# A two-layer decoder trunk: a first group of four outputs, other loads, an input order with two groups ahead of the up-projections, and scores on 128 rows

## The chip, the cores and the metric

The kernel runs on one core of a Trainium2 chip, in one launch for the whole trunk. The metric is the device time of that launch in microseconds (us), the median of several runs.

## The reference

The trunk has 2 layers; the batch is 1, the sequence 256 positions, the model width 2048, all in float32. Cut to what matters here, a layer is:

```python
h = rmsnorm(x, g_mix)
z = h @ w_in
zq, zkv, zkr, sc_b, sc_c, sc_h, cf_a, cf_g, rq, rk, rv, rg = split_cols(z, ...)
y_a = attention(zq, zkv, zkr)
y_b = sc_b * causal_dwconv(sc_c * sc_h, w_sc)
u   = causal_dwconv(cf_a * sigmoid(cf_g), w_cf, b_cf)
y_c = silu(layernorm(u))
y_d = silu(rg) * rmsnorm(retention(rotate(rq), rotate(rk), rv))
x = x + concatenate([y_a, y_b, y_c, y_d]) @ w_o
uf = causal_dwconv(rmsnorm(x) @ w_up, w_ffn_conv)
x = x + (silu(gate) * up) @ w_down
x = x + (p @ w_pe) * sigmoid(rmsnorm(x) @ w_pg)
```

The attention first makes low-rank inputs: q comes from a norm of zq (512 columns) and `w_q_up`, k and v from a norm of zkv (256) and `w_kv_up`. Each of its 4 heads has 128 columns without position and 64 that are rotated by it; the rotated 64 of k come from zkr and are the same for all heads. A score is thus a product over 128 + 64 numbers. A retention head, 4 of them too, has q and k of 64 rotated numbers, and its scores are multiplied by a decay table. `w_cf` has 31 taps on 512 channels.

## The kernel before

**Layout and precision.** Everything is kept with channels on the 128 partitions and the 256 positions along the free axis. A float32 product is made of three: weights and inputs are each split in a rounded part `hi` and a rest `lo`, and hi x hi, hi x lo and lo x hi are summed in PSUM. An input tile S holds its hi half in columns 0 to 255 and its lo half in columns 256 to 511. So each 128x128 block of weights is used twice (`linear`, line 308): its `hi` by one matmul of 512 columns, its `lo` by one of 256. An output of 128 channels of the input projection takes 16 blocks.

**The weight stream.** The host writes all blocks in the order of their use, as `in_groups` and the loops of line 50 on give it. They come 16 at a time, 1 MB a load, in three buffers `raw`. ACT casts 8 blocks at once to `hi` (`conv_hi`, line 262, three buffers), and DVE subtracts that from `raw` to give `lo` (`conv_lo`, line 276, five buffers). `use` (line 293) is called ahead of each matmul and issues the conversions that the buffers have room for, so that the order of the matmuls sets the order of the conversions on ACT and DVE.

**The groups.** `in_groups` (line 88) lists the groups of the input projection: four pairs cf0 to cf3 (a half of `cf_a` with its gate), zkv, zkr, zq0, zq1, then "up" (the up-projections, `do_up`, line 593), rk, rq, rv, rg0, rg1, and the short convolution's. A group makes two outputs (zkr one, rv four) in one accumulator of two PSUM banks; there are two of these and four single banks `ps` for everything else. In layer 0, cf0 runs while x arrives: `pre` (line 856) splits two input tiles at a time, as `norm_split` (line 485 on) writes it, and squares them for the norm of line 485 on. `evac` (line 366) brings an accumulator out: ACT copies one half, DVE adds the other and multiplies by the norm's row.

**Side work.** What lies between the groups is written as generators in chains of `Bg` (line 146): chain A holds the attention with its norms and the tables of cosines and sines (`rope_tables`, line 438), C the 31 taps of each tile of the convolution, R the retention, N the first norm. `linear` calls `bg.tick()` after each step of two blocks per output, and a tick lets each chain go a step of its rate on: 1 for most, 0.4 for C (`CF_RATE`), 0.25 for the tables, which also wait for eight ticks first. Each instruction so issued stands in its engine's queue behind the last matmul or `lo` conversion issued before it, and the queues run in that order. All DVE instructions and matmuls go through `Paced` and show as line 135 in the profile.

**Scores.** `rope` (line 472) rotates: ACT copies the halves crosswise, DVE multiplies both by the tables and adds. The rotated k of zkr is made twice, on rows 0 to 63 and 64 to 127 (the group's columns are doubled, line 90), since the tile `qr` holds two heads, one on each half of the rows. `t_attn` (line 628) makes a head's scores in two pieces, of 128 and 256 columns, each of two float32 matmuls, one on 128 rows and one on the 64 of its head:

```python
T.matmul(ps[:, c0:c0 + n], qn[j][:, s, qs], kn[j][:, s, 0:n], start=True, stop=False)
T.matmul(ps[:, c0:c0 + n], qr[pr, j, qs], kr[pr, 0, 0:n], start=False, stop=True)
```

`t_ret` (line 774) makes a retention head's in two matmuls on 64 rows each. For the norm of k, `t_zkr` (line 559) squares rows 0 to 63 alone.

**First loads.** They are issued from line 215 on. SP's queue takes 8 KB of `vt` (the vectors of gains and taps; these columns are the gains of the first norm), then the first weights and the 8 tiles of x, 512 KB and 256 KB each, in turn. POOL's queue takes `ident`, the positions, `ropec`, the other 466 KB of `vt` and the decay table `dect`.

Of the kernel before, what the change touches and what calls it, by code (L numbers as in the profile page):

```python
# [17 lines left out]
P = 128  # L18
# [17 lines left out]
GRP = 32  # L36
NHI, NLO = 3, 5
# [50 lines left out]
def in_groups():  # L88
    r = lambda a: np.arange(a, a + P)
    rd = np.concatenate([np.arange(O_ZKR, O_ZKR + 64)] * 2)  # L90
    out = [("cf%d" % i, [r(O_CA + i * P), r(O_CG + i * P)]) for i in range(4)]
    out += [("zkv", [r(O_ZKV), r(O_ZKV + P)]),
            ("zkr", [rd]),
            ("zq0", [r(O_ZQ), r(O_ZQ + P)]),
            ("zq1", [r(O_ZQ + 2 * P), r(O_ZQ + 3 * P)]),
            ("up", None),
            ("rk", [r(O_RK), r(O_RK + P)]),
            ("rq", [r(O_RQ), r(O_RQ + P)]),
            ("rv", [r(O_RV + i * P) for i in range(4)]),
            ("rg0", [r(O_RG), r(O_RG + P)]),  # L100
            ("rg1", [r(O_RG + 2 * P), r(O_RG + 3 * P)])]
# [86 lines left out]
def trunk(ctx: ExitStack, tc: tile.TileContext, ws, xT, pT, pos, vec, dec, ident_d, rope_c, out):  # L188
# [25 lines left out]

    vt = one.tile([P, L * NV], F32, tag="vt", name="vt")
    nc.sync.dma_start(vt[:, 0:KD], vec[:, 0:KD])
    st = {"dma": 2, "hi": 0, "lo": 0, "b": 0, "uh": 0, "ul": 0}
    raws, his, los = {}, {}, {}
    NRAW = 3
    raws[0] = tl("raw", [P, CB * P], F32, NRAW, wp)  # L220
    x = [one.tile([P, 2, S], F32, tag="x%d" % i, name="x%d" % i) for i in range(8)]
    raws[1] = tl("raw", [P, CB * P], F32, NRAW, wp)
    for kind, i in (("w", 0), ("x", 0), ("w", 1), ("x", 1), ("x", 2), ("w", 2), ("x", 3), ("x", 4), ("w", 3),
                    ("x", 5), ("x", 6), ("x", 7)):
        if kind == "x":
            nc.sync.dma_start(x[i], xT[i])
        else:
            o = slice(i % 2 * HB * P, (i % 2 + 1) * HB * P)
            nc.sync.dma_start(raws[i // 2][:, o], ws[i // 2][:, o])
# [9 lines left out]
    ones = one.tile([P, P], F32, tag="ones", name="ones")  # L239
    V.memset(ones, 1.0)  # L240
# [19 lines left out]


    def conv_hi(h):
        h = min(h, nhalf - 1)
        while st["hi"] <= h:
            i = st["hi"]
            while st["dma"] <= min(i // 2 + 1, ws.shape[0] - 1):
# [205 lines left out]
    def rope(dst, src, n, ct, sn, tag):  # L472

        sw = tl(tag, [P, n, S], F32, 3)
# [3 lines left out]
        V.tensor_tensor(dst, src, bc(ct, n), op=ALU.mult)  # L478
        V.tensor_tensor(dst, dst, sw, op=ALU.add)
# [47 lines left out]
    def layer_fwd(li, nrm, a, nxt):  # L527
# [31 lines left out]
        def t_zkr(z):  # L559
            sq = tl("krsq", [64, S], F32)  # L560
            A.activation(sq, z[0:64, 0], AF.Square)
# [4 lines left out]
            kr = tl("kr", [P, 1, S], F32)  # L566
            rope(kr, kg, 1, tabs["cm"], tabs["sm"], "m")
# [60 lines left out]
        def t_attn(ksq, qsq, qrsq, kn, vv, qn, qg):  # L628
# [4 lines left out]
            col_sums(psk, 8, [st_["krsq"]])  # L633
# [33 lines left out]
            for hh in range(4):  # L667
# [6 lines left out]
                pr = slice(64 * s, 64 * s + 64)  # L674
# [386 lines left out]
```

## Time and profile before

| what | value |
|---|---|
| time, median of 3 runs | 2411.74 us (2410.95 to 2411.9) |
| the profiled execution's own time | 2411.2 us |
| its span, first to last instruction | 2409.4 us |
| PE (matmul) busy | 2386.6 us, 99% |
| DVE busy | 1752.0 us, 73% |
| ACT busy | 1316.6 us, 55% |
| POOL busy | 10.7 us |
| moved by DMA | 443.33 MB, mean 184 GB/s |
| weights `hi`: matmuls of 512 columns in `linear` | 6560, busy 1543.5 us |
| weights `lo`: matmuls of 256 columns in `linear` | 6432, busy 841.3 us |
| `lo` conversions on DVE, 128x1024 | 830, busy 1000.8 us |

The page gives each engine's busy time over the span, and the groups of instructions that cost most. A busy share is an average over all stages. The views of the trace that are quoted below cut it in time: the list of waits says for what an engine stood idle and how long, the timeline gives start and length of runs of like instructions on an engine. In a timeline matmuls overlap, since a matmul starts before the one ahead has ended; so time is read there from start to start.

### The profile page before, as it was taken

The numbers are of one execution on the slowest core, as the hardware profiler recorded it, in microseconds if no ns is written. First come the engines' busy times: TensorE is split into PE (matmuls) and PEld (weight loads), VectorE is DVE, ScalarE is ACT, GpSimd is POOL, SyncE is SP. The second block draws the span as 40 slices with busy tenths as digits, with TensorE's granted clock in tenths as the row PEclk, the third lists the DMA queues.
The fourth block names the chain that finished last, engine by engine and source line by source line (L and its number), as shares of the span: only waits on it lengthen the run. The fifth ranks groups of instructions, "written<-read, shape, count | busy, mean of one in ns | idle before, by whom it ended". The sixth has DMA issues, their size and how long they took to land.

```text
span 2409.4 us, 34651 instructions
## 1 busy us (share of the span) xinstructions
PE 2386.6 (99%) x13808; PEld 2101.9 (87%) x13808; DVE 1752.0 (73%) x2722; ACT 1316.6 (55%) x1896; POOL 10.7 (0%) x35
## 2 busy tenths in 40 slices
PE   8999999999999999999999999999999999999999
PEld 7888888888888888888989888888888888888888
DVE  7977977777656777666788779777775567776665
ACT  6665565555445555555556665655554455555453
POOL 0000000000000000000000000000000000000000
PEclk9999999999999999999999999999999999999999
DMA  6533555555555555555554444555555555555554
GB/s 242 180 141 144 177 191 192 180 198 182 192 192 186 199 177 196 188 190 186 185 189 174 157 145 175 192 191 183 191 188 193 191 188 189 186 191 191 192 187 146
DMA packets 63332, 443.33 MB, mean 184 GB/s; under 512 B 7249, under 2 KB 7505, under 8 KB 10305
## 3 DMA queue, kind: packets, MB, share of 16 engines
q1 hardware_dynamic: 62640, 439.39, 50.8%
q8 instruction: 108, 1.77, 0.3%
q0 software_dynamic: 528, 1.73, 0.2%
q14 instruction: 56, 0.45, 0.1%
HBM read 438.99 MB, written 2.10 MB: 183 GB/s over the span
## 4 chain that ended last, share of the span: by engine, by line
PE 93%; DVE 4%; ACT 1%; issue 1%; DMA 1%; SPq 0%; POOLq 0%; ACTq 0%; DVEq 0%
PE acc L135 90%; PE ps L135 4%; DVE lo L135 2%; DVE cfu L135 1%; DMA x<-xT 0%; DVE s L135 0%; DVE e L135 0%; ACT dg L426 0%; DMA m<-pT 0%; ACT hi L272 0%; DVE S L135 0%; ACT m L476 0%; DVE m L135 0%; DVE x L135 0%; ACT e L369 0%
## 5 line engine op out<-in xcount | busy, mean ns | idle before, releaser
L135 PE MATMUL acc<-S,hi 128*128 128x512 f32 x6560 | 1543.5, 387 | 12.1 <-DVE S L135 10.8
L135 PEld LDWEIGHTS acc<-S,hi 128*128 128x128 f32 x6560 | 1203.7, 188 | 241.7 <-DVE S L135 11.3
L135 DVE TENSOR_TENSOR lo<-raw,hi 128x1024 fp32r<-128x1024 f32 x830 | 1000.8, 1220 | 205.1 <-ACT hi L272 169.9
L272 ACT CAST hi<-raw 128x1024 fp32r<-128x1024 f32 x830 | 872.1, 1053 | 357.3 <-PE acc L135 311.2
L135 PE MATMUL acc<-S,lo 128*128 128x256 f32 x6432 | 841.3, 283 | 1.3 <-DVE lo L135 1.3
L135 PEld LDWEIGHTS acc<-S,lo 128*128 128x128 f32 x6432 | 817.5, 192 | 23.1 <-DVE lo L135 1.9
L369 ACT COPY e<-acc 128x512 f32<-128x512 f32 x138 | 80.5, 584 | 417.9 <-PE acc L135 417.6
L135 DVE TENSOR_TENSOR e<-acc,e 128x512 f32<-128x512 f32 x138 | 94.9, 688 | 259.0 <-ACT e L369 258.9
L135 DVE SCALAR_TENSOR_TENSOR m<-e,vt,m 128x255 f32<-128x255 f32 (+1 forms) x352 | 146.1, 477 | 0.0
L904 ACT COPY e<-acc 128x512 f32<-128x512 f32 x64 | 37.6, 587 | 147.0 <-PE acc L135 147.0
L135 DVE TENSOR_TENSOR x<-x,acc 128x512 f32<-128x512 f32 x64 | 44.0, 688 | 99.8 <-ACT e L904 99.8
L135 DVE SCALAR_TENSOR_TENSOR cfu<-cfpad,vt,cfu 128x256 f32<-128x256 f32 x240 | 115.3, 481 | 1.6
L135 DVE TENSOR_TENSOR e<-e,rrow 128x512 f32<-128x512 f32 x138 | 94.8, 687 | 4.4
L942 ACT ACTIVATE m<-e,vt 128x256 f32<-128x256 f32 x176 | 79.5, 500 | 0.0
L135 DVE TENSOR_TENSOR S<-m,S 128x256 fp32r<-128x256 f32 x92 | 38.9, 425 | 40.5 <-ACT S L380 40.5
L380 ACT CAST S<-m 128x256 fp32r<-128x256 f32 x92 | 37.2, 406 | 53.5 <-DVE m L135 53.5
L135 DVE TENSOR_TENSOR x<-x,e 128x512 f32<-128x512 f32 (+1 forms) x82 | 55.6, 677 | 2.2
L426 ACT ACTIVATE dg<-ident,s8r 128x128 fp32r<-128x128 f32 x104 | 33.4, 391 | 31.3 <-DVE s8r L135 31.3
L135 PE MATMUL acc<-hi,S 128*128 128x512 f32 x144 | 47.4, 398 | 0.0
L384 ACT ACTIVATE S<-x,vt 128x256 fp32r<-128x256 f32 x96 | 42.9, 496 | 1.7 <-DMA x<-xT 1.6
L135 DVE SCALAR_TENSOR_TENSOR S<-x,vt,S 128x256 fp32r<-128x256 f32 x96 | 42.0, 479 | 0.9 <-ACT S L384 0.9
L947 ACT ACTIVATE m<-m 128x256 f32<-128x256 f32 x88 | 36.0, 410 | 3.7 <-DVE m L135 3.7
(161 smaller groups left out, 693.7 us busy)
## 6 DMA issues: line engine op xcount, KB each, us to landing
raw<-ws SPq DMA_DIRECT2D x413, 1024.0 KB, 4.8
raw<-ws SPq DMA_DIRECT2D x4, 512.0 KB, 9.5
x<-xT SPq DMA_DIRECT2D x8, 256.0 KB, 10.1
out<-x SPq DMA_DIRECT2D x7, 256.0 KB, 3.7
dect<-dec POOLq DMA_DIRECT2D x1, 512.0 KB, 9.8
m<-pT POOLq DMA_DIRECT2D x4, 128.0 KB, 3.5
vt<-vec POOLq DMA_DIRECT2D x1, 466.0 KB, 8.3
out<-x SPq DMA_DIRECT2D x2, 128.0 KB, 1.7
```

Of the source, the lines that this page charges most:

```text
L135: r = fn(*a, **k)
L272: A.copy(his[i], raws[i // 2][:, (i % 2) * HB * P:(i % 2 + 1) * HB * P])
L369: A.copy(out_, t[:, 0:nmt, S:2 * S])
L380: A.copy(dst[:, 0:S], src)
L384: A.activation(dst[:, 0:S], src, AF.Identity, scale=g)
L426: A.activation(dg[:, i, tt], ident, AF.Identity, scale=hl[i][:, c0 + tt:c0 + tt + 1])
L904: A.copy(e, t[:, :, S:2 * S])
L942: A.activation(y[:, m], u[:, m], AF.Identity, scale=w(2))
L947: A.activation(y[:, 0], y[:, 0], AF.Silu)
```

## The change

It does six things.

1. The first group makes the four outputs of cf0 and cf1 at once (`cf01`), two in an accumulator and two in single banks `ps`; in layer 0 a step is one input tile and four weight blocks, and the squares of the first norm come two tiles at a time, half of them after the group.
2. The groups cf2 and cf3 come behind zq1, ahead of the up-projections.
3. `WARM` = 12 matmuls of `ones` by `ones`, whose results are never read, are the first on PE.
4. The 8 KB of `vt` go alone on POOL's queue. SP's queue takes first 4 blocks of weights, the two halves of the first x tile, 4 more blocks, then x tiles and weights in turn, and behind them `ident`, `ropec`, the rest of `vt` and the positions; `dect` follows with the sixth conversion. The first 8 blocks are converted in two pieces of 4.
5. The tables wait for six ticks and then go a step every tick.
6. The rotated q of retention and the rotated k of attention are written to two tiles, one with rows 64 to 127 zero, one with rows 0 to 63 zero (POOL fills them), and all scores are products over 128 rows. The squares of zkr run on 128 rows, and the sum over them takes a column of `ropec` that selects half.

```diff
+WARM = 12
 def in_groups():
-    out = [("cf%d" % i, [r(O_CA + i * P), r(O_CG + i * P)]) for i in range(4)]
-    out += [("zkv", [r(O_ZKV), r(O_ZKV + P)]),
-            ("zkr", [rd]),
...
-            ("zq1", [r(O_ZQ + 2 * P), r(O_ZQ + 3 * P)]),
-            ("up", None),
+    cf = lambda i: [r(O_CA + i * P), r(O_CG + i * P)]
+    out = [("cf01", cf(0) + cf(1)),
+           ("zkv", [r(O_ZKV), r(O_ZKV + P)]),
+           ("zkr", [rd]),
...
+           ("zq1", [r(O_ZQ + 2 * P), r(O_ZQ + 3 * P)]),
+           ("cf2", cf(2)),
+           ("cf3", cf(3)),
+           ("up", None),
...
+    V.memset(ones, 1.0)
     vt = one.tile([P, L * NV], F32, tag="vt", name="vt")
-    nc.sync.dma_start(vt[:, 0:KD], vec[:, 0:KD])
+    nc.gpsimd.dma_start(vt[:, 0:KD], vec[:, 0:KD])
...
+    load_w(0, 4)
+    for m in range(2):
+        nc.sync.dma_start(x[0][:, m], xT[0][:, m])
+    load_w(4, 8)
+    for i in range(1, 6):
+        nc.sync.dma_start(x[i], xT[i])
+        load_w(8 * i, 8 * i + 8)
+    for i in range(6, 8):
+        nc.sync.dma_start(x[i], xT[i])
...
-    nc.gpsimd.dma_start(ident, ident_d)
+    nc.sync.dma_start(ident, ident_d)
-    nc.gpsimd.dma_start(ropec, rope_c)
-    nc.gpsimd.dma_start(vt[:, KD:], vec[:, KD:])
+    nc.sync.dma_start(ropec, rope_c)
+    nc.sync.dma_start(vt[:, KD:], vec[:, KD:])
+    nc.sync.dma_start(posi, pos.broadcast_to([P, S]))
...
-    nc.gpsimd.dma_start(dect, dec)
...
+    for _ in range(WARM):
+        wm = pst()
+        T.matmul(wm[:, 0:P], ones, ones, start=True, stop=True)
...
+    def pieces(i):
+        n = HB * P // (2 if i == 0 else 1)
+        return [slice(j, j + n) for j in range(0, HB * P, n)]
+    def c_first(i):
+        return i == 5
...
+            if c_first(i):
+                nc.sync.dma_start(dect, dec)
             his[i] = tl("hi", [P, HB * P], F32R, NHI, wp)
-            A.copy(his[i], raws[i // 2][:, (i % 2) * HB * P:(i % 2 + 1) * HB * P])
+            for o in pieces(i):
+                A.copy(his[i][:, o], src(i)[:, o])
...
     def rope(dst, src, n, ct, sn, tag):
         V.tensor_tensor(sw, sw, bc(sn, n), op=ALU.mult)
-        V.tensor_tensor(dst, src, bc(ct, n), op=ALU.mult)
-        V.tensor_tensor(dst, dst, sw, op=ALU.add)
+        if isinstance(dst, list):
+            V.tensor_tensor(src, src, bc(ct, n), op=ALU.mult)
+            for q, d in enumerate(dst):
+                r = slice(64 * q, 64 * q + 64)
+                G.memset(d[64 - 64 * q:128 - 64 * q], 0.0)
+                V.tensor_tensor(d[r], src[r], sw[r], op=ALU.add)
+        else:
+            V.tensor_tensor(dst, src, bc(ct, n), op=ALU.mult)
+            V.tensor_tensor(dst, dst, sw, op=ALU.add)
...
-            col_sums(psk, 8, [st_["krsq"]])
+            col_sums(psk, 8, [(st_["krsq"], ropec[:, 3:4])])
...
-                    T.matmul(ps[:, c0:c0 + n], qr[pr, j, qs], kr[pr, 0, 0:n], start=False, stop=True)
+                    T.matmul(ps[:, c0:c0 + n], qr[:, j, qs], kr[:, s, 0:n], start=False, stop=True)
...
-                T.matmul(ps[:, 0:S], rk[pr, j, 0:P], rq[pr, j, :], start=True, stop=True)
-                T.matmul(ps[:, S:384], rk[pr, j, P:S], rq[pr, j, P:S], start=True, stop=True)
+                T.matmul(ps[:, 0:S], rk[:, j, 0:P], rq[s][:, j, :], start=True, stop=True)
+                T.matmul(ps[:, S:384], rk[:, j, P:S], rq[s][:, j, P:S], start=True, stop=True)
...
+            if kind == "cf01":
+                t = pacc.tile([P, 2, 512], F32, tag="acc", name=nm("acc"))
+                t2 = [pst(), pst()]
+                linear(h, 4, AB_IN, ps=[t[:, 0, :], t[:, 1, :]] + t2, pre=pre)
...
-                    bg.add("A", 0.25, wait_ticks(8))
-                    bg.add("A", 0.25, rope_tables())
+                    bg.add("A", 1, wait_ticks(6))
+                    bg.add("A", 1, rope_tables())
```

**First place: the start of PE's queue.** `acc` are accumulators, `ps` single banks, S_0, S_1 the first split input tiles; x2 stands for two matmuls of the row. Before:

```order
L1056 UNCONDITIONAL_BRANCH
L135 MATMUL acc_140<-S_0_4_123,hi_145 128x512 x2
L135 MATMUL acc_140<-S_0_4_123,lo_153 128x256 x2
L135 MATMUL acc_140<-S_1_5_124,hi_145 128x512 x2
L135 MATMUL acc_140<-S_1_5_124,lo_153 128x256 x2
L135 MATMUL acc_140<-S_2_6_125,hi_145 128x512 x2
L135 MATMUL acc_140<-S_2_6_125,lo_153 128x256 x2
```

With the change:

```order
L1102 UNCONDITIONAL_BRANCH
L139 MATMUL ps_126<-ones 128x128
L139 MATMUL ps_128<-ones 128x128
...
L139 MATMUL ps_148<-ones 128x128
L139 MATMUL acc_167<-S_0_16_150,hi_174 128x512 x2
L139 MATMUL ps_168<-S_0_16_150,hi_174 128x512
L139 MATMUL ps_169<-S_0_16_150,hi_174 128x512
L139 MATMUL acc_167<-S_0_16_150,lo_181 128x256 x2
L139 MATMUL ps_168<-S_0_16_150,lo_181 128x256
L139 MATMUL ps_169<-S_0_16_150,lo_181 128x256
L139 MATMUL acc_167<-S_1_17_151,hi_174 128x512 x2
```

The unused matmuls stand ahead, and each input tile now serves four matmuls of each kind in place of two, before the next tile is wanted.

**Second place: DVE's queue in the groups behind the convolution's first.** `lo` are the conversions that PE waits for, `cfu` the taps, `e` evacuations, `tab...` the tables, m and s temporaries. Before, in cf2 and zkv:

```order
L135 TENSOR_TENSOR lo_488<-raw_428,hi_470 128x1024
L135 SCALAR_TENSOR_TENSOR cfu_60_350<-cfpad_107,vt,cfu_60_350 128x256 x6
L135 TENSOR_TENSOR e_518<-acc_427,e_518 128x512
L135 SCALAR_TENSOR_TENSOR cfu_60_350<-cfpad_107,vt,cfu_60_350 128x256
L135 TENSOR_TENSOR e_518<-e_518,rrow_318 128x512
L135 SCALAR_TENSOR_TENSOR cfu_60_350<-cfpad_107,vt,cfu_60_350 128x256
L135 TENSOR_TENSOR lo_530<-raw_456,hi_528 128x1024
L135 SCALAR_TENSOR_TENSOR cfu_60_350<-cfpad_107,vt,cfu_60_350 128x256
L135 TENSOR_TENSOR cfpad_111<-e_518,c_522 128x256
L135 SCALAR_TENSOR_TENSOR cfu_60_350<-cfpad_107,vt,cfu_60_350 128x256
L135 TENSOR_TENSOR lo_543<-raw_456,hi_541 128x1024
```

With the change, in zkr and zq0:

```order
L139 TENSOR_TENSOR e_584<-acc_451,e_584 128x512
L139 TENSOR_TENSOR tabsr<-tabcr,m_547 128x256
L139 TENSOR_TENSOR e_584<-e_584,rrow_432 128x512
L139 TENSOR_SCALAR tabcr<-tabsr 128x256
L139 TENSOR_TENSOR lo_593<-raw_481,hi_591 128x1024
L139 TENSOR_SCALAR m_547<-tabcr 128x256
L139 TENSOR_SCALAR tabsr<-tabsr 128x256
L139 TENSOR_TENSOR tabcr<-tabcr,m_547 128x256
L139 TENSOR_SCALAR tabsm<-tabsm,ropec 128x256
L139 TENSOR_SCALAR tabcr<-tabcr 128x256
L139 TENSOR_TENSOR m_601<-m_601 128x256
L139 TENSOR_SCALAR tabsr<-tabsr,ropec 128x256
```

The rows of the tables, which stood one by one between conversions and taps, now stand several in a row between two conversions.

**Third place: PE's queue ahead of the up-projections.** `acc_966` before is zq1, `acc_1028` with the change cf3; S_4_131 and S_4_112 are the first tiles of the normed zkv, which the up-projection of k and v reads. Before:

```order
L135 MATMUL acc_966<-S_10_14_133,lo_971 128x256 x2
L135 MATMUL acc_966<-S_11_15_134,lo_971 128x256 x2
L135 MATMUL acc_1097<-S_4_131_860,hi_1007 128x256 x2
L135 MATMUL acc_966<-S_12_16_135,lo_992 128x256 x2
L135 MATMUL acc_966<-S_13_17_136,lo_992 128x256 x2
L135 MATMUL acc_966<-S_14_18_137,lo_992 128x256 x2
L135 MATMUL acc_966<-S_15_19_138,lo_992 128x256 x2
L135 MATMUL acc_966<-S_15_19_138,hi_990 128x512 x2
L135 MATMUL acc_1097<-S_4_131_860,lo_1009 128x256
L135 MATMUL acc_1097<-S_4_131_860,hi_1007 128x256 x2
L135 MATMUL acc_1097<-S_4_131_860,lo_1009 128x256
```

With the change:

```order
L139 MATMUL acc_1028<-S_12_28_162,lo_1045 128x256 x2
L139 MATMUL acc_1028<-S_13_29_163,lo_1045 128x256 x2
L139 MATMUL acc_1028<-S_14_30_164,lo_1045 128x256 x2
L139 MATMUL acc_1028<-S_15_31_165,lo_1045 128x256 x2
L139 MATMUL acc_1028<-S_15_31_165,hi_1043 128x512 x2
L139 MATMUL acc_1126<-S_4_112_670,hi_1058 128x256 x2
L139 MATMUL acc_1126<-S_4_112_670,lo_1060 128x256
L139 MATMUL acc_1126<-S_4_112_670,hi_1058 128x256 x2
```

The same step now comes behind cf3, two groups after zq1, and its `lo` matmuls no longer stand behind matmuls of zq1.

## Rows read from the trace of the kernel before

**Rows 1.** The page: the span, and PE's busy time, share and instructions.
```profile
span 2409.4 us, 34651 instructions
...
PE 2386.6 (99%) x13808; PEld 2101.9 (87%) x13808; DVE 1752.0 (73%) x2722; ACT 1316.6 (55%) x1896; POOL 10.7 (0%) x35
```

**Rows 2.** PE's waits, 0 to 125 us: us in total, times, longest.
```profile
PE acc L135 <- DVE S L135: 10.8, 3, 8.5
PE acc L135 <- DVE lo L135: 1.3, 2, 1.1
PE acc L135 <- ACT S L604: 1.3, 1, 1.3
PE ps L135 <- DVE m L135: 1.2, 1, 1.2
```

**Rows 3.** Timeline of PE from 8 us: start, length, line, operation [idle before].
```profile
8.53 1.22 PE L135 MATMUL acc<-S,hi 128*128 128x512 f32 x2 [8.53 <-DVE S L135]
...
13.49 1.22 PE L135 MATMUL acc<-S,hi 128*128 128x512 f32 x2 [2.03 <-DVE S L135]
...
17.48 0.63 PE L135 MATMUL acc<-S,hi 128*128 128x512 f32 x2
...
18.96 0.64 PE L135 MATMUL acc<-S,hi 128*128 128x512 f32 x2
...
19.67 0.62 PE L135 MATMUL acc<-S,hi 128*128 128x512 f32 x2
```

**Rows 4.** Stretch 10 to 20 us: length, busy PE, PEld, DVE, ACT, POOL, clock, DMA, GB/s.
```profile
10.00:20.00 10.00, 7.97 (x31) 6.57 (x31) 7.86 (x14) 8.38 (x16) 0.00 (x0) 1.00 1.04 403
```

**Rows 5.** DVE's waits, 43 to 120 us.
```profile
DVE cfpad L135 <- ACT c L721: 1.2, 1, 1.2
DVE s L135 <- PE ps L135: 0.4, 1, 0.4
DVE S L135 <- ACT S L384: 0.4, 1, 0.4
DVE m L135 <- PE ps L135: 0.4, 1, 0.4
```

**Rows 6.** Timeline of all engines from the start.
```profile
0.84 0.17 DVE L135 MEMSET ones<- 128x128 f32 x1 [0.84 <-PEq L1051]
...
8.00 0.87 DVE L135 SCALAR_TENSOR_TENSOR S<-x,vt,S 128x256 fp32r<-128x256 f32 x2
...
38.10 6.99 PE L135 MATMUL acc<-S,hi 128*128 128x512 f32 x30
```

**Rows 7.** DMA issues, 0 to 30 us: count, KB each, median us to landing.
```profile
vt<-vec POOLq DMA_DIRECT2D x1, 466.0 KB, 8.3
...
ident<-ident POOLq DMA_DIRECT2D x1, 64.0 KB, 4.9
vt<-vec SPq DMA_DIRECT2D x1, 8.0 KB, 1.7
```

**Rows 8.** Timeline of PE: attention scores, then retention; float32 matmuls have two records each.
```profile
194.82 0.38 PE L135 MATMUL ps<-S,S 128*128 128x128 f32 x2
...
196.80 0.73 PE L135 MATMUL acc<-S,hi 128*128 128x512 f32 x2
...
206.43 0.92 PE L135 MATMUL ps<-m,S 128*128 128x256 f32 x4
207.10 0.70 PE L135 MATMUL acc<-S,hi 128*128 128x512 f32 x2
...
207.73 0.92 PE L135 MATMUL ps<-S,S 64*128 64x256 f32 x4
208.58 0.96 PE L135 MATMUL acc<-S,hi 128*128 128x512 f32 x3
```

**Rows 9.** Timeline of DVE from 59.8 us, layer 0.
```profile
59.80 1.22 DVE L135 TENSOR_TENSOR lo<-raw,hi 128x1024 fp32r<-128x1024 f32 x1
60.94 0.29 DVE L135 TENSOR_SCALAR m<-m 128x256 f32<-128x256 f32 x1
61.14 0.48 DVE L135 SCALAR_TENSOR_TENSOR cfu<-cfpad,vt,cfu 128x256 f32<-128x256 f32 x1
61.53 0.42 DVE L135 SCALAR_TENSOR_TENSOR tabsm<-m,m 128x256 f32<-128x256 f32 x1
61.87 0.48 DVE L135 SCALAR_TENSOR_TENSOR cfu<-cfpad,vt,cfu 128x256 f32<-128x256 f32 x1
```

More of the change, by code (lines that the diff above doesn't have):

```diff
@@ L212, in pst @@
         return pmis.tile([P, 512], F32, tag="ps", name=nm("ps"))
+    ones = one.tile([P, P], F32, tag="ones", name="ones")
+    V.memset(ones, 1.0)
     vt = one.tile([P, L * NV], F32, tag="vt", name="vt")
-    nc.sync.dma_start(vt[:, 0:KD], vec[:, 0:KD])
-    st = {"dma": 2, "hi": 0, "lo": 0, "b": 0, "uh": 0, "ul": 0}
+    nc.gpsimd.dma_start(vt[:, 0:KD], vec[:, 0:KD])
+    st = {"dma": 3, "hi": 0, "lo": 0, "b": 0, "uh": 0, "ul": 0}
     raws, his, los = {}, {}, {}
     NRAW = 3
-    raws[0] = tl("raw", [P, CB * P], F32, NRAW, wp)
@@ L221, in trunk @@
     x = [one.tile([P, 2, S], F32, tag="x%d" % i, name="x%d" % i) for i in range(8)]
[L222 to L229, printed above, removed]
+    for i in range(3):
+        raws[i] = tl("raw", [P, CB * P], F32, NRAW, wp)
@@ L232, in trunk @@
-    posi = tl("e", [P, S], I32, 3)
-    nc.gpsimd.dma_start(posi, pos.broadcast_to([P, S]))
+    nc.sync.dma_start(ident, ident_d)
     ropec = one.tile([P, 5], F32, tag="ropec", name="ropec")
-    nc.gpsimd.dma_start(ropec, rope_c)
-    nc.gpsimd.dma_start(vt[:, KD:], vec[:, KD:])
+    nc.sync.dma_start(ropec, rope_c)
+    nc.sync.dma_start(vt[:, KD:], vec[:, KD:])
+    tabs = {}
+    for nme in ("cm", "sm", "cr", "sr"):
+        tabs[nme] = one.tile([P, S], F32, tag="tab" + nme, name="tab" + nme)
@@ L237, in trunk @@
+    posi = tabs["sr"].bitcast(I32)
+    nc.sync.dma_start(posi, pos.broadcast_to([P, S]))
     dect = one.tile([P, 4, S], F32, tag="dect", name="dect")
-    nc.gpsimd.dma_start(dect, dec)
-    ones = one.tile([P, P], F32, tag="ones", name="ones")
-    V.memset(ones, 1.0)
     ones_r = one.tile([P, P], F32R, tag="ones_r", name="ones_r")
@@ L565, in t_zkr @@
             yield
-            kr = tl("kr", [P, 1, S], F32)
-            rope(kr, kg, 1, tabs["cm"], tabs["sm"], "m")
+            kr = tl("kr", [P, 2, S], F32)
+            rope([kr[:, q:q + 1] for q in range(2)], kg, 1, tabs["cm"], tabs["sm"], "m")
             st_["kr"] = kr
@@ L851, in layer_fwd, with pre @@
             n = len(cols)
[L852 to L866 removed]
+            if kind == "cf01":
+                pre = None
+                if li == 0:
+                    def pre(k):
+                        if k % 2 == 0:
+                            norm_split(nrm, k // 2)
+                            if k >= 8:
+                                norm_square(nrm, (k - 8) // 2)
+                t = pacc.tile([P, 2, 512], F32, tag="acc", name=nm("acc"))
+                t2 = [pst(), pst()]
+                linear(h, 4, AB_IN, ps=[t[:, 0, :], t[:, 1, :]] + t2, pre=pre)
+                if li == 0:
+                    for i in range(4, 8):
+                        norm_square(nrm, i)
+                    bg.add("N", 1, norm_end(nrm))
+                bg.flush("N")
+                if li == 0:
+                    bg.add("A", 1, wait_ticks(6))
+                    bg.add("A", 1, rope_tables())
+                zs = [evac_in(t, 2, AB_IN), tl("e", [P, 2, S], F32, 3)]
+                for m in range(2):
+                    evac(t2[m][:, None, :], 1, AB_IN, zs[1][:, m:m + 1], nrm.row)
+                for i in range(2):
+                    for _ in t_glu(zs[i], i):
+                        pass
+                    bg.add("C", CF_RATE, t_cf(i))
+                continue
+            t = linear(h, n, AB_IN)
             if kind in ("rg0", "rg1"):
```

47 lines of the change are left out of this document (18 added, 29 removed).

## The prediction, made before the changed kernel ran

> **What bounds the kernel now.** The page first: TensorE (PE) is busy for 2386.6 of the 2409.4 us of the span [rows 1], so the time is PE's queue, and only what shortens that queue or fills a hole in it counts. The holes come next, from PE's list of waits: up to 125 us it waits 10.8 us for the split of the input, 1.3 for `lo` conversions, 1.3 for ScalarE (ACT) at line 604 and 1.2 for a VectorE (DVE) sum [rows 2]. Third, the timeline of PE's start: the first matmul runs at 8.53 us, there is a hole of 2.03 us before 13.49, and the steps are slow until 17.48 [rows 3]. A step is two 512-column and two 256-column matmuls: 18.96 to 19.67 is 0.71 us, while the three steps from 13.49 to 17.48 took 1.33 each. So a block (one matmul of each width) costs 0.357 us at the 2.4 GHz level and nearly twice that at the 1.2 GHz level, although the window from 10 to 20 us gives the granted clock as 1.00 [rows 4]. Before it rose, PE had worked without a hole from 13.49 on. Last, DVE: from 43 to 120 us it waits for 2.4 us in all, once for 1.2 and three times for 0.4 [rows 5]. There DVE runs as its queue is written, and that is where a faster start can be lost again.
>
> **Part 1, the start.** Before, DVE makes the `lo` half of the first x tile from 8.00 us on [rows 6], behind the conversion of 1024 weights per partition, and the first matmul waits for it. The change cuts these pieces in half and puts only them at the head of SP's queue, takes the tables off POOL's queue, and leaves 8 KB of vt there. From POOL the rest of vt took 8.3 us to land beside the loads of x [rows 7]. The small vt is the first on POOL's queue now, but no row shows how long it alone takes from there: no less than the 1.7 us that SP's small vt took, no more than the 8.3 of the long one [rows 7]. Nearest is ident, 64 KB, first on that queue, 4.9 us, and vt is smaller, so I take 4: issued at 1.2, there at 5.3. ACT 0.45, DVE about 0.5 and the hand-overs put the first matmul at 6.4 us, 2.1 earlier (3.9 and 9.5 to 10 at the ends).
>
> Twelve unused matmuls fill PE from the memset of `ones` (0.84 + 0.17) on [rows 6]. In f32, which the trace lists as two records a matmul, 384 columns took 0.67 us at the full rate (206.43 to 207.10 [rows 8]), so 128 cost 0.22, so 0.43 at half: they reach to about 6.2 if the clock stays low and end sooner if it rises; either way PE has worked for 4 to 5 us by 6.4. I take the whole slow stretch as gone. Its price: five slow steps, two from 8.53 on and three from 13.49 on, at 1.33 in place of 0.71, 3.1 us. (Nothing of it gone is the other end.)
>
> With four outputs a weight block feeds as before, but each x tile now feeds twice the work: 8 blocks, 2.86 us of PE. In the 10 us from 10 on ACT was busy 8.38 and DVE 7.86 [rows 4], in which about four x tiles and their weights were prepared, some 2.1 us a tile. So they keep up after the second x tile, where I count 1.2 us of waiting for the second conversion in place of the hole of 2.03 [rows 3]. The 64 blocks cost 22.8 us. Before, the third group began at 38.10 [rows 6], with 1.2 us of the norm's small matmuls and waits in it that now come later. After: 6.4 + 22.8 + 1.2 = 30.4. **Gain 38.1 - 1.2 - 30.4 = 6.5 us.**
>
> **Part 2, DVE takes some back.** The rope tables went one step every fourth tick and now go every tick, all inside DVE's work for zkr and zq0 (second place of the order). Start to start a conversion costs DVE 1.14 us, a tap 0.39, a table instruction 0.20 or 0.34 [rows 9]. From the norm's last sum to zq0's fourth conversion its queue now holds 8 conversions (9.1 us), 33 table instructions (8.7), 12 taps (4.8), 13 evacuations and gates priced likewise (5.3) and small ones (1.9): 29.8 us without waits. I add 4 us for waits: 0.6 for the copy out of PSUM, 1.3 for the norm's sums, 0.6 for its row, 1.5 for the sigmoid and its table load (the same chain cost 1.2 at the sigmoid before [rows 5]). Begun at 29.4, this ends at 63.5 to 64. PE wants that conversion at 30.4 + 0.5 (the norm's small matmuls) + 11.4 (zkv, 32 blocks) + 5.7 (zkr) + 6.8 + 2.9 (zq0) = 57.7. It is 6 us late, and the order gives PE only six `hi` matmuls of the next group meanwhile (1.4 us, of which 0.4 only shifts). **Loss 5.2 us.** Later DVE is ahead again: zq1 to cf3 are 12 conversions in 31.7 us of DVE's queue against 34.3 us of PE.
>
> **Part 3, the waits before the up-projections.** Between zq1 and kv now stand cf2 and cf3, 22.9 us of PE work (third place), so zkv's and zq's norms are done when the up-projections want them. The four waits, 1.3 + 1.3 + 1.2 us [rows 2], go: **gain 3.8 us**. Late next: zkv's row inside zq1, whose diagonal DVE finishes at about 67.8, a wait of up to 1 us; and ACT at the up-projections, for which PE waited at line 604 before [rows 2] and which has the last two evacuations of cf3 on its queue besides. I take off 0.1 here and keep 2 us for the range. In layer 1 there are no tables and no start to make up; I count nothing there. Sum of parts 1 to 3: 6.5 - 5.2 + 3.8 - 0.1 = 5.0 us.
>
> **Part 4, scores on 128 rows.** A head's scores go 128 rows, 64, 128, 64: from 194.82 to 196.80, 1.98 us, and the next 512-column matmul takes 0.11 more than its 0.23 [rows 8]: 2.09 us for 768 columns. The product with the values, 384 columns all on 128 rows, takes 0.68 (206.43 to 207.10) and 0.09 after it; 384 more columns, without another entry or exit, I put at 0.64. So all on 128 rows a head costs 1.41 us by these rows. Per switch of row count about 0.2 us goes: 0.1 in the matmul before it, 0.1 in the one after. I take 0.62 rather than 0.68 a head, for entry waits that stay: 8 heads, 5.0 us. A retention head on 64 rows: 207.73 to 208.58 and 0.11 after, 0.96 against 0.77: 0.2 x 8 = 1.6 us. DVE gets one more instruction at each of four ropes (0.34 to 0.6), POOL six fills; both queues are idle enough there. **Gain 6.6 us**; ends 0 (the switch costs nothing of its own) and 7.5.
>
> The Trainium skill, TensorEngine Tiling, section Key Properties, says that a change of tiling mode drains TensorE; its section When to Use Tiling recommends two row tiles where the contracted size is 64 or less, for up to twice the speed, and by that this part would lose. The trace sides with the first: 384 columns on 64 rows take 0.85 us, on 128 rows 0.68 [rows 8].
>
> The dect load and vt's rest go through SP behind x: 5 MB ahead of them, and in the window from 10 to 20 us 403 GB/s moved [rows 4]; even at half that rate they are there by 30, before their first readers. The mask column for krsq costs nothing, the late taps (6 fewer by the up-projections) end before the last half of the output projection.
>
> **Sum.** 5.0 + 6.6 = 11.6 us off the profiled execution's 2411.2: 2399.6. The runs' median, 2411.74, is 0.5 higher, so the forecast is **2400 us**.
>
> **Rivals.**
> (a) DVE's table work is hidden after all, since it may use the holes that I count as waits, or the weight buffers hold enough: part 2 costs nothing, 2395 us. For it: five `lo` buffers are 14 us of PE work. Against: DVE had no slack there before either.
> (b) DVE takes the whole start: waits for sigmoid, sine and row add up to 10 us, or vt lands late at the first step. Then only part 4 is left, 2411.7 - 6.6 = 2405.
> (c) The switch of rows is not what the extra 0.1 us are; part 4 gives nothing: 2406.7.
> (d) Slower: a 64-row product is the cheaper one, and zeros on the other rows double it. Each of the 16 heads has 384 columns of it, 0.85 us [rows 8]: 13.6 us more, part 4's gain gone, parts 1 to 3 kept: 2411.7 + 13.6 - 5.0 = 2420. It decides from 0.31 us per head on (5.0 / 16). Rows 8 speak against it. Only the advice above, from the Trainium skill's TensorEngine Tiling, would have it so.
> (e) The start does not move, since vt on POOL's queue lands as late as the long one did: first matmul at 10, part 1 falls to about 3 us and part 2 with it: 2401 to 2403, inside the range.
>
> **How the numbers follow.** The forecast's case with (e) 0.60, (a) 0.15, (b) 0.17, (c) 0.06, (d) 0.02. A measurement of this kernel tells about 0.2%, 4.8 us, from no change: 2406.9. (c) lies on that line, so two thirds of it go to no change: faster 0.94, the same 0.04, slower 0.02. The range takes in (a) with part 4 at its upper end, 2394, and (b), 2405; it leaves out (c), (d) and the tails, under 2 in 10.
>
> **What would show it.** First real matmul near 6.4 and steps of 1.43 us for four blocks from the start; the third group, zkv, at about 30.4; PE waiting for `lo` 4 to 6 us between 54 and 66; no waits of over 0.5 us at the up-projections; a head's scores in 1.3 to 1.5 us. Wrong if zkv starts later than 33, if the `lo` waits in zq0 are under 2 or over 8 us, or if a head still takes 1.9.

## The result, and the profile after

The changed kernel takes 2398.77 us (median of 6 runs, 2398.28 to 2399.71), the kernel before 2411.73 in the same comparison: 0.9947 of it, 95% interval 0.9935 to 0.996. It is 13.0 us faster; 2400 was forecast, 2394 to 2405 the range. The profiled execution took 2398.78 us, its span is 2397.0. So the total came within 1.2 us. Its parts did not all come so, and the rest of this document is about them.

The page of the changed kernel, its span and its busy times:

```profile
span 2397.0 us, 34732 instructions
...
PE 2381.7 (99%) x13832; PEld 2107.2 (88%) x13832; DVE 1752.7 (73%) x2731; ACT 1318.8 (55%) x1900; POOL 11.6 (0%) x39
```

Against [rows 1] the span is 12.4 us shorter, of which PE's busy time gives 4.9 and its idle time the rest; the 5.3 us of unused matmuls count as busy here. PE's list of waits up to 125 us shows what idle time is left:

```profile
PE acc L139 <- DVE e L139: 4.7, 2, 4.4
PE acc L139 <- ACT hi L298: 2.0, 1, 2.0
PE ps L139 <- DVE ones L139: 1.1, 1, 1.1
```

Of the four lines of [rows 2] none is left at its place: the first wait for the split of the input is filled by unused matmuls (1.1 us until `ones` is set), and the waits for `lo`, for the row sum and for ACT at line 604 (now 639) are gone. New is a wait of 4.4 us for `e`, an evacuation on DVE. The timeline of PE's start:

```profile
1.06 5.28 PE L139 MATMUL ps<-ones 128*128 128x128 f32 x24 [1.06 <-DVE ones L139]
6.11 0.71 PE L139 MATMUL acc<-S,hi 128*128 128x512 f32 x2
...
11.13 0.74 PE L139 MATMUL acc<-S,hi 128*128 128x512 f32 x2 [1.98 <-ACT hi L298]
...
13.08 1.05 PE L139 MATMUL acc<-S,hi 128*128 128x512 f32 x2
...
15.64 0.90 PE L139 MATMUL acc<-S,hi 128*128 128x512 f32 x2
...
17.32 0.63 PE L139 MATMUL acc<-S,hi 128*128 128x512 f32 x2
```

The first matmul that counts runs at 6.11 us (8.53 before, [rows 3]). The unused ones reach until 6.1, at the low level throughout (24 records, 0.22 us each from start to start, twice the 0.11 of a 128-column record at the full rate). The first two steps, of four blocks each, run at full rate from 6.11 to 8.98. Then PE stands idle for 1.98 us, and the step at 13.08 takes 2.56 us where one from 17.32 on takes 1.40: the clock has fallen again. The windows (their columns as in [rows 4], the granted clock is the third figure from the end) say so too, and once more behind the long wait at 50 us:

```profile
11.00:17.00 6.00, 5.82 (x22) 4.66 (x23) 5.89 (x9) 6.00 (x13) 0.00 (x0) 0.72 1.04 402
17.00:30.00 13.00, 13.00 (x78) 11.41 (x77) 11.65 (x18) 9.21 (x15) 0.00 (x0) 1.00 0.96 360
...
55.00:62.00 7.00, 7.00 (x22) 5.57 (x22) 5.48 (x14) 2.30 (x4) 0.00 (x0) 0.60 0.00 0
```

The long wait itself, in PE's timeline, and what DVE does meanwhile:

```profile
32.74 1.98 PE L139 MATMUL acc<-S,hi 128*128 128x512 f32 x8
...
44.45 0.63 PE L139 MATMUL acc<-S,hi 128*128 128x512 f32 x2
...
50.15 0.39 PE L139 MATMUL acc<-S,hi 128*128 128x512 f32 x1
54.96 6.77 PE L139 MATMUL acc<-S,hi 128*128 128x512 f32 x17 [4.42 <-DVE e L139]
61.57 0.50 PE L139 MATMUL ps<-ones,m 128*128 128x1 f32 x4
```

```profile
45.84 1.36 DVE L139 TENSOR_TENSOR e<-e,rrow 128x512 f32<-128x512 f32 x3
48.45 0.43 DVE L139 TENSOR_TENSOR cfpad<-e,c 128x256 f32<-128x256 f32 x1 [1.26 <-ACT c L755]
...
54.13 0.69 DVE L139 TENSOR_TENSOR e<-acc,e 128x512 f32<-128x512 f32 x1
```

The third group, zkv, starts at 32.74 us (38.10 before, [rows 6]). zq0's first matmul wants an accumulator; there are two, and the one whose turn it is holds zkv, which PE finished by 44.9. DVE evacuates it at 54.13, since its queue runs in order and holds most of the tables, the row of the first norm, both gates and six taps ahead of it. PE starts at 54.96, and its 17 matmuls until 61.57 take 0.39 us each in place of 0.23, 2.7 us in all. So this one place costs 7.1 us.

Further on, scores and retention (PE, compare [rows 8]):

```profile
192.01 0.38 PE L139 MATMUL ps<-S,S 128*128 128x128 f32 x2
...
193.13 1.75 PE L139 MATMUL acc<-S,hi 128*128 128x512 f32 x6
...
204.06 0.81 PE L139 MATMUL ps<-S,S 128*128 128x256 f32 x4
204.63 1.63 PE L139 MATMUL acc<-S,hi 128*128 128x512 f32 x6
```

A head's scores now take 1.12 us from start to start and leave 0.19 to the matmul behind them, 1.31 us together, where they took 2.09: 0.77 less. A retention head takes 0.57 and leaves 0.09.

### The profile page after: what moved, and what is told of

The parts are those of the page before. It is cut to its first block, busy times and chain, and to the rows that moved or that the text cites. A ratio compares the mean times of both kernels' runs of the same rounds, so it can differ in the third digit from the quotient of the medians.

```text
span 2397.0 us, 34732 instructions
## 1 busy us (share of the span) xinstructions
PE 2381.7 (99%) x13832; PEld 2107.2 (88%) x13832; DVE 1752.7 (73%) x2731; ACT 1318.8 (55%) x1900; POOL 11.6 (0%) x39
## 4 chain that ended last, share of the span: by engine, by line
PE 93%; DVE 2%; ACT 1%; issue 0%
PE acc L139 90%; PE ps L139 4%; DVE lo L139 1%; DVE cfu L139 0%; DVE s L139 0%; ACT m L504 0%; DVE e L139 0%; DVE S L139 0%; ACT hi L298 0%; DVE m L139 0%; ACT dg L453 0%; ACT e L396 0%; DVE nacc L139 0%; ACT S L407 0%; DVE kr L139 0%
## 5 line engine op out<-in xcount | busy, mean ns | idle before, releaser
L139 PE MATMUL acc<-S,hi 128*128 128x512 f32 (+1 forms) x6496 | 1533.6, 387 | 6.7 <-DVE e L139 4.7
L139 DVE TENSOR_TENSOR lo<-raw,hi 128x1024 fp32r<-128x1024 f32 (+1 forms) x831 | 1000.2, 1218 | 204.4 <-ACT hi L298 168.5
L298 ACT CAST hi<-raw 128x1024 fp32r<-128x1024 f32 (+1 forms) x831 | 872.6, 1052 | 366.9 <-PE acc L139 302.3
L139 DVE TENSOR_TENSOR e<-e,rrow 128x512 f32<-128x512 f32 (+1 forms) x140 | 94.9, 680 | 4.3
```

What stands on the lines that cost most here:

```text
L139: r = fn(*a, **k)
L298: A.copy(his[i][:, o], src(i)[:, o])
```

## The experiments

All but the first are edits of the changed kernel, so their times are read against 2398.8; the first is read against 2411.7.

### Which part gives what: the rows alone, and everything but the rows

The first kernel is the one before with part 4 of the prediction alone: two tiles for the rotated k and q, each with half its rows zero, and all scores on 128 rows. The second is the changed kernel with that undone.

```diff
-                    T.matmul(ps[:, c0:c0 + n], qr[pr, j, qs], kr[pr, 0, 0:n], start=False, stop=True)
+                    T.matmul(ps[:, c0:c0 + n], qr[:, j, qs], kr[:, s, 0:n], start=False, stop=True)
```

> The kernel before with the scores of both attentions on 128 rows (part 4 of the prediction) and nothing else of the change. Theory A, read from the changed kernel's trace: from the start of rk to the end of a layer's input part the change saves 5.7 us in layer 0 and about 5.8 in layer 1, and nearly all of that is the rows: 2400 to 2402 us. Theory B, the prediction's price of 6.6 us: 2405, and the other 5 us after rk come from the moved groups and loads. Nothing saved (rival c): 2411.7.

> The changed kernel with the scores back on 64 rows; start, order, loads and tables as changed. Theory A: the start and the order are worth only 1 to 2 us together, so 2409.5 to 2411. Theory B: they are worth 5.0 us or more as predicted, so 2405.5 to 2407.

Measured: 2404.27 us (2403.24 to 2404.55) and 2406.51 us (2405.05 to 2408.46); as ratios to the kernel before 0.9967 (0.9954 to 0.9979) and 0.9978 (0.9969 to 0.9987). The rows give 7.5 us alone and 7.7 on top of the rest, the rest 5.2 alone: 7.5 and 5.2 are 12.7 of the 13.0. Theory A, drawn from one profiled execution of the changed kernel (it starts the group rk at 118.9 us, only 0.6 earlier than before), falls. That execution had both falls of the clock in it; in the one that was profiled without the rows, the clock stayed at 1.00 from 11 to 17 us, fell less behind the long wait (0.84 from 55 to 62 us in place of 0.60), and rk started at 116.1. One execution is not enough to price a stretch in which the clock falls in some and not in others.

With the rows alone PE's waits over the whole kernel are longer at two places (in the kernel before 2.3 us for the diagonals, `dg`, and 1.2 for DVE's `m`):

```profile
PE ps L135 <- ACT dg L426: 3.6, 8, 1.2
PE ps L135 <- DVE m L135: 3.0, 3, 1.2
```

### The tables behind zkv's norm

```diff
-                if li == 0:
-                    bg.add("A", 1, wait_ticks(6))
-                    bg.add("A", 1, rope_tables())
...
                 bg.add("A", 1, t_zkv(z))
+                if li == 0:
+                    bg.add("A", 1, rope_tables())
```

> The changed kernel with the tables' generator put behind zkv's norm in chain A, in place of ahead of it. Theory A: the 4.4 us that PE waits at 50.5 us for zkv's evacuation come from table instructions ahead of the norm's row and of that evacuation on DVE; both move ahead of them, the wait goes, and with it the 2.6 us of slow matmuls behind it: 2391.5 to 2394. Theory B, the prediction's sum of DVE work: DVE has as much to do as before, the conversions of zq1 or cf2 come late instead, 4 to 5 us are lost elsewhere: 2397 to 2400.

Measured: 2398.88 us (2396.82 to 2399.02), no gain. The wait at 50 us is gone; these stand in its place in PE's timeline (the last column is the idle time and what ended it):

```profile
49.07 0.58 PE L139 MATMUL ps<-ones,m 128*128 128x1 f32 x4 [0.57 <-DVE m L139]
...
75.99 1.22 PE L139 MATMUL acc<-S,lo 128*128 128x256 f32 x8 [1.17 <-DVE lo L139]
...
79.60 3.86 PE L139 MATMUL acc<-S,hi 128*128 128x512 f32 x14 [1.92 <-ACT hi L298]
...
92.60 3.48 PE L139 MATMUL acc<-S,hi 128*128 128x512 f32 x14 [0.72 <-ACT hi L298]
...
103.33 0.50 PE L139 MATMUL acc<-S,hi 128*128 128x256 f32 x2 [1.50 <-ACT S L639]
```

They add up to 5.9 us. The wait of the kernel before, at the evacuation of the up-projections, is back, and conversions to `hi` come late in two places. Where they stand in ACT's queue:

```profile
76.84 0.42 ACT L493 ACTIVATE tabsr<-tabsr 128x256 f32<-128x256 f32 x1 [0.86 <-DVE tabsr L139]
...
78.52 1.03 ACT L298 CAST hi<-raw 128x1024 fp32r<-128x1024 f32 x1
...
91.02 0.59 ACT L396 COPY e<-acc 128x512 f32<-128x512 f32 x1 [4.15 <-PE acc L139]
```

The first comes behind sines, of which one waited for DVE's table rows, and behind a copy of an evacuation; the next ones run from 91.50 on, behind a copy that waited for PE. How much of the delay is this order and how much the buffers that DVE frees is not shown. The execution with these rows is the fastest of the five, and its clock did not fall behind the hole at 9 us: zkv starts 1.8 us earlier than in the changed kernel's profile (30.99), rk 2.7 earlier (116.24). So of the 7.1 us at the long wait only 0.9 are left as a gain by rk. This is theory B: moved, for the most part, and not removed.

### The hole at 9 us filled, and no unused matmuls at all

```diff
+FILL = 9
...
                     def pre(k):
+                        for _ in range(FILL if k == 2 else 0):
+                            T.matmul(pst()[:, 0:P], ones, ones, start=True, stop=True)
```

> The changed kernel with 9 more unused 128-column matmuls ahead of the third step, where PE stands idle from 8.98 to 11.13 us. Theory A: the granted clock falls behind that hole (0.83 in the window from 10 to 20 us), and the slow steps until 16.2 us cost 3 us; with the hole filled the clock stays and the first group ends 2.5 to 3 us earlier. If DVE's delay at 50 us only shifts with it, the kernel takes 2395.8 to 2396.3; if DVE sets the end of that wait by itself, the gain is lost there: 2398.5 to 2399. Theory B, the fall does not come from the hole: the slow steps remain, 2398.5 to 2399.5.

Measured: 2396.74 us (2395.96 to 2397.78), 2.0 less than the change. The granted clock from 11 to 17 us in its profile:

```profile
11.00:17.00 6.00, 6.00 (x37) 5.17 (x36) 6.00 (x9) 6.00 (x12) 0.00 (x0) 1.00 1.04 401
```

It stays. In the changed kernel's profile the slow steps cost 2.0 us: 1.95, 2.56 and 1.68 in place of three times 1.40. From profile to profile zkv starts 1.5 us earlier (31.25 in place of 32.74); a part of the difference is that the third step, now behind the unused matmuls, starts at 11.29 in place of 11.13. Theory A, if a little smaller than I had put it; the wait at 50 us stayed (4.4 us), and zq0 and rk start 1.5 us earlier too (53.47 and 117.42), so the gain was carried through it.

The other way round, `WARM = 0`:

> The changed kernel without the twelve unused matmuls. Theory A, the prediction's: they save slow steps; without them the two steps ahead of the hole take 2.66 us each in place of 1.39, so 2.5 us more, and the clock rises behind the hole only: 2401 to 2402. Theory B: the third step waits for weights that ACT converts at 10 to 11 us whatever came before, so two slow steps from 6.1 end at 11.4 and only fill the hole; PE then works without a pause, and the clock rises no later than it does now: 2398 to 2399.5.

Measured: 2397.74 us (2397.15 to 2398.63), 1.0 less than with them, with ranges that overlap. The start of PE's timeline:

```profile
6.05 1.22 PE L139 MATMUL acc<-S,hi 128*128 128x512 f32 x2 [6.05 <-DVE S L139]
...
8.78 1.05 PE L139 MATMUL acc<-S,hi 128*128 128x512 f32 x2
...
11.34 0.87 PE L139 MATMUL acc<-S,hi 128*128 128x512 f32 x2
...
13.17 0.62 PE L139 MATMUL acc<-S,hi 128*128 128x512 f32 x2
```

Two slow steps reach from 6.05 to 11.34, just when the third step's weights are ready (11.13 with the unused matmuls). PE has no hole, and from 12 us on the steps are fast and stay so. The twelve unused matmuls bought two fast steps that PE then waited behind. Theory B.

### The order of before

cf2 and cf3 back ahead of zkv, all else as changed:

> The changed kernel with cf2 and cf3 back ahead of zkv. Theory A, the parts priced apart: the 3.8 us of waits ahead of the up-projections come back, but 7 us at 50 us (the wait for zkv's evacuation and the slow steps behind it) go: 2395.5 to 2397. Theory B, DVE's queue as a whole bounds the stretch from 30 to 105 us: what is not lost at 50 us is lost further on, and the waits ahead of the up-projections come on top: 2399 to 2402.

Measured: 2395.67 us (2393.77 to 2396.06): 3.1 us faster than the change. Moving the two groups costs time. Theory A, and this is its row (DVE, then PE):

```profile
53.05 0.68 DVE L139 TENSOR_TENSOR e<-acc,e 128x512 f32<-128x512 f32 x1
...
53.88 2.08 PE L139 MATMUL acc<-S,hi 128*128 128x512 f32 x8 [1.25 <-DVE e L139]
```

DVE evacuates at nearly the same time as before the edit, 53.05 in place of 54.13. But the group between the one evacuated and the one that waits is now a full one, 32 blocks, and not zkr with its 16, so PE comes 2 us later and waits 1.25 us in place of 4.4, without a fall of the clock. And the waits ahead of the up-projections do not come back with the old order, which I had expected in both theories; waits of 0.9 and 1.1 us for conversions to `hi`, at 61.9 and 93.6 us, stand there in their place. So theory A's sum, 3.8 lost and 7 won, met the time without being right in its terms. What took the waits ahead of the up-projections away is shown by the same kernel with the tables at their old rate:

```diff
-                    bg.add("A", 1, wait_ticks(6))
-                    bg.add("A", 1, rope_tables())
+                    bg.add("A", 0.25, wait_ticks(8))
+                    bg.add("A", 0.25, rope_tables())
```

> The changed kernel with the order of before and the tables at their old rate, a step every fourth tick behind eight ticks. Theory A: in the order of before it is the tables' rate that took the waits ahead of the up-projections away (zkv's norm stood behind the tables in chain A): they come back, 2 to 3.8 us, 2397.5 to 2399.5. Theory B: the earlier start took them away: 2395 to 2396.5.

Measured: 2397.2 us (2396.0 to 2397.96), 1.5 more. Some of that may be the clock: in this profile it fell behind the hole at 9 us, in the one at the new rate it did not (last section). PE's waits up to 130 us:

```profile
PE acc L139 <- DVE lo L139: 2.4, 2, 2.1
...
PE acc L139 <- ACT S L639: 1.3, 1, 1.3
```

Two lines of [rows 2] are there again. At the old rate the tables end in the groups where zkv's norm stands behind them in chain A. In the order of before it is thus the tables' earlier and faster run that takes these waits away, and the move is not needed for it. Whether the move alone, with the tables at their old rate, would take them away too was not measured.

### The tables on POOL

```diff
-            V.tensor_scalar(ang, posf, ropec[:, fi:fi + 1], None, op0=ALU.mult)
+            G.tensor_scalar(ang, posf, ropec[:, fi:fi + 1], None, op0=ALU.mult)
...
-            V.scalar_tensor_tensor(r, y, -6.25, ang, op0=ALU.mult, op1=ALU.add)
+            G.tensor_scalar(c, y, -6.25, None, op0=ALU.mult)
+            G.tensor_tensor(r, c, ang, op=ALU.add)
```

> The changed kernel with the tables computed on POOL (their fused instructions written as two, 37 in place of 31), the sines behind zkv's norm; DVE's queue loses 33 instructions, 8.7 us. Theory B, DVE's sum bounds the stretch from 30 to 105 us: the wait at 50 us goes and nothing comes back later, 2391.5 to 2394.5. Theory A, single places in the order bound it: as with the tables behind zkv's norm, waits appear at conversions and at the up-projections instead: 2396 to 2399. If POOL is so slow that the sines wait for it, or if it slows DVE beside it: 2399 or more.

> The tables on POOL and the hole at 9 us filled. If the two gains add (the hole alone gave 2.0 us): 2 us less than with the tables on POOL alone, 2389.5 to 2392.5. If DVE still sets the end of the stretch, no more than 0.5 us less.

Measured: 2412.1 us (2410.97 to 2412.82) and 2411.95 us, the whole gain lost. POOL took about 1 us for one of these instructions, and worked until 60 us. ACT's queue had the sines ahead of the first norm's diagonal, so that the diagonal waited for POOL, and with it PE, 18.9 us. This is the last case of the first expectation. One row of POOL's timeline, and behind it two of ACT's and one of PE's:

```profile
32.37 0.74 POOL L478 TENSOR_TENSOR tabsm<-tabcm,tabsm 128x256 f32<-128x256 f32 x1
```

```profile
58.86 0.42 ACT L493 ACTIVATE tabsr<-tabsr 128x256 f32<-128x256 f32 x1 [12.32 <-POOL tabsr L489]
...
60.27 1.26 ACT L453 ACTIVATE dg<-ident,s8r 128x128 fp32r<-128x128 f32 x4
```

```profile
61.00 0.58 PE L139 MATMUL ps<-dg,ones_r 128*128 128x256 f32 x1 [18.92 <-ACT dg L453]
```

With the last clamps kept on DVE, so that the sines can't come before them:

> The changed kernel with all but the last clamps of the tables on POOL, and the clamps on DVE behind zkv's norm, so that the sines can't stand ahead of the first norm's diagonal on ACT as they did with the tables on POOL. DVE loses 27 of the 33 instructions. Theory B, DVE's sum bounds the stretch: the 4.4 us wait and the slow steps behind it go and do not come back, 2391.5 to 2394.5. Theory A, the places in the order bound it: 2396 to 2399. If POOL slows DVE beside it (conversions took 1.31 us in place of 1.22, and small ones 0.3 to 0.6 in place of 0.15, while it worked): 1 to 3 us more than the theory that holds.

Measured: 2398.29 us (2396.9 to 2399.38), no clear gain, although DVE had 27 instructions less. The wait for the evacuation is gone, others have come, and DVE itself is slower beside POOL (from 25 to 62 us a tap takes 0.62 us on the mean in place of the 0.48 of [rows 9], a conversion 1.32 in place of 1.22; two of the slower ones are shown):

```profile
PE ps L139 <- DVE m L139: 2.6, 1, 2.6
PE ps L139 <- ACT dg L453: 1.1, 1, 1.1
```

```profile
50.62 0.96 DVE L139 SCALAR_TENSOR_TENSOR cfu<-cfpad,vt,cfu 128x256 f32<-128x256 f32 x1
51.51 1.41 DVE L139 TENSOR_TENSOR lo<-raw,hi 128x1024 fp32r<-128x1024 f32 x1
```

Two things went with this edit, the lighter queue and the slower instructions, so it does not tell whether DVE's sum or the places in its order bound the stretch. That stays open. The Trainium skill (Trainium Architecture — The Big Picture, What this means for kernel authors) says that VectorE and GpSimd contend for a pair of ports that they share; the slower rows agree.

### The best of them

The order of before and the hole filled:

> The changed kernel with the order of before (cf2 and cf3 ahead of zkv, 2395.7 alone) and the hole at 9 us filled. If the clock fell behind the hole in only some executions of the order of before (in its profile it did not, 1.00 from 11 to 17 us), the fill gives 0 to 1 us and less scatter: 2394.5 to 2395.7. If the hole costs as much as in the changed kernel, where the fill gave 2.0: 2393 to 2394.5.

Measured: 2394.17 us (2393.94 to 2394.29), 0.9923 of the kernel before (0.991 to 0.9937), 4.6 us faster than the change and the best version here. The fill gave 1.5 us, more than the 0 to 1 that the clock of one profile had suggested. Beside the changed kernel with the hole filled (2396.74) it prices the move of cf2 and cf3 again, without the hole: 2.6 us. Its waits over the whole kernel, but for the first 1.1 us and those under 1 us:

```profile
PE acc L140 <- ACT hi L299: 2.1, 3, 1.1
PE ps L140 <- ACT dg L454: 1.4, 4, 0.5
PE acc L140 <- DVE e L140: 1.3, 1, 1.3
```

A last experiment on its 1.3 us, the tables at half the rate:

> The changed kernel with the order of before, the hole at 9 us filled, and the tables a step every second tick (behind six ticks, as now), so that they end with cf3. Beside the same kernel at a step every tick (2394.2), whose PE waits 1.25 us for an evacuation at 53.5 us and 1.1 for conversions until 61.5. Theory A, places in the order bound this stretch: the evacuation and the conversions come earlier on DVE, 1 to 2.3 us less, 2392 to 2393.2. Theory B, the saturated queue only moves its wait: 2393.9 to 2394.8. If zkv's norm then stands behind the tables, as at a step every fourth tick (2397.2 without the fill): 2395 to 2396.

Measured: 2395.1 us (2394.45 to 2395.51), 0.9 more, the third case. The wait for the evacuation is gone, and in its place PE waits for conversions and again at the up-projections (waits up to 130 us):

```profile
PE acc L140 <- DVE lo L140: 2.6, 4, 1.2
PE acc L140 <- ACT S L640: 1.3, 1, 1.3
```

## Why the prediction was right, and where it was wrong

**Right: the whole, and its two halves.** Parts 1 to 3 were put at 5.0 us and part 4 at 6.6; the runs show 5.2 and 7.5 to 7.7. That the first half came so near is luck: parts 1 and 2 gave less than forecast, and gains behind rk that were counted as nothing made up for it (part 3 below). The first matmul at 6.4 was 6.11, vt's 8 KB from POOL's queue took 3.5 us where 4 was taken, and rivals (a), (c), (d) and (e) did not come: the loss at 50 us is there, the rows give 7.5, and vt is early. Rival (b), DVE taking the whole start, came true in the profiled execution up to rk (0.6 us saved), but not in the runs' sum.

**Part 1: the slow stretch did not go.** "I take the whole slow stretch as gone" failed. The prediction had a hole of 1.2 us behind the second x tile and priced it as waiting only; it was 1.98 us, and the clock fell behind it. Zkv started at 32.74 in place of 30.4: 0.3 less from the first matmul, 0.9 more in the hole (2.15 us from the end of the second step to the start of the third), 2.0 more in slow steps, 0.3 less in the other steps. By the prediction's own sign, zkv later than 33, this part was 0.3 us from being wrong. The unused matmuls, put at 3.1 us, were worth nothing (2397.74 without them), and nine more at the hole were worth 2.0.

**Part 2: the engine and the group right, the instruction and the price's make-up not.** A loss of 5.2 us was forecast for a late `lo` conversion in zq0, between 54 and 66 us, with DVE's sum as its cause. PE did stop there, at zq0, for DVE, but at 50.5 us for the evacuation of zkv, 4.4 us, and the list of waits has none for `lo`: by the prediction's own sign, `lo` waits under 2 us, this part was wrong. I had counted the evacuations' time in DVE's queue and not asked when PE needs the buffer that each frees. The 2.7 us of slow steps behind it were not in the sum. That 5.2 was forecast and 7.1 came is thus not a confirmation of its working, in which 29.4 + 29.8 + 4 is 63.2 besides, and not 63.5 to 64. The tables moved behind zkv's norm (2398.88) show the kind of bound that part 2 spoke of: take the wait away at one place, and it comes back at others.

**Part 3: the gain was there, its cause was not the move.** 3.8 us of waits went, as forecast. But in the order of before they go too, by the tables' rate, and the move itself costs 3.1 us (2395.67 without it; 2.6 where the hole is filled in both). Zkr stands between zkv and zq0 in either order; the move brings the two to the place behind cf01, where DVE is late with an evacuation. There the group behind the one to be evacuated is zkr, with 16 blocks, where it was cf3, with 32. At rk the sum of parts 1 to 3 was 0.6 us in the changed kernel's profile, 2.3 less by part 1 and 1.9 less by part 2 than forecast. Against that stand gains that I had counted as nothing: in the kernel without the rows the lead at rk, 3.4 us, grows to 6.2 at the end (spans and timelines of the profiled executions). Of those 2.8 us some 0.8 are waits for the diagonals (line 426, now 453) on ACT that are shorter; the rest was not traced.

**Part 4: right, somewhat under-sized.** A score head gave 0.77 us, not 0.62, and a retention head 0.39 (0.3 behind it and within, 0.09 in the matmul ahead), not 0.2: 6.2 + 3.1 = 9.3 us on PE, of which the runs show 7.5. In the profile with the rows alone PE is busy for 10.1 us less than before (2376.5), while its waits behind 125 us are 2.9 longer, twice 0.87 us for DVE's `m` and the rest for the diagonals, both shown with the first experiment. The prediction put such waits at nothing. That a change of the row count costs time of its own is now shown from the other side: with all products on 128 rows the excess at each switch is gone. Between the switches nothing changes: inside each of the eight retention heads the records on 64 rows start 0.216 and 0.109 us apart, as on 128 rows, and the excess is at the first (0.32 in place of 0.215) and behind the last (0.20 in place of 0.03). Of the two statements of the Trainium skill that the prediction quoted from TensorEngine Tiling, the one in Key Properties agrees.

## What to carry to other kernels

Where an engine's queue is full, ask of each evacuation when the next user of its buffer comes: a short group behind a long one halves the time that the evacuation has. Price a wait of PE with the slow steps that may stand behind it: behind waits of 4.4 us the clock fell here each time, behind shorter ones only in some executions. Before filling PE ahead of its first data, look whether the data for the next step will be there; here a slow start without a hole was as good as a fast one with one. And try the removal of a wait in a run, and do not price it by its row alone: in a saturated stretch a wait that is removed at one place tends to stand at the next.

## What the runs showed of the hardware

- The granted clock does not fall behind every hole of 2 us. Behind the hole at 9 us it was 1.00 where PE stood idle for 1.50, 1.62, 2.25 or 2.30 us, and 0.72 for 1.80, 1.98 or 2.50 us. From 11 to 17 us it was 1.00 behind a hole of 2.30 us (the order of before, the first row) and 0.72 behind one of 1.80 (the same with slow tables, the second):

```profile
11.00:17.00 6.00, 5.55 (x29) 4.50 (x30) 5.63 (x9) 6.00 (x12) 0.00 (x0) 1.00 1.04 403
```

```profile
11.00:17.00 6.00, 6.00 (x25) 5.11 (x26) 6.00 (x9) 6.00 (x12) 0.00 (x0) 0.72 1.04 402
```

With the hole filled it was 1.00 in all four kernels profiled.

- Unused matmuls run at the low level for a time that differs from one execution to the next: the same twelve took 4.3 to 5.5 us in the eleven profiles that have them.

- Float32 products on 64 rows between products on 128 cost time where the row count changes: 1.18 us in place of 0.88 for a retention head, up to the second matmul behind it. Between the changes they run as fast as those on 128 rows.

- POOL is slow at element-wise work on 128x256 float32 (0.4 to 2.4 us for one instruction of the tables, where DVE takes 0.3 to 0.4), and DVE is slower beside it.
